# Four transposes in one PSUM bank, and maxima over partitions by way of DRAM, in a hybrid attention layer

## The chip, the cores and the metric

The kernel runs on one core of one Trainium2 chip. The metric is the device time of one execution in microseconds (us). Five instruction queues matter: TensorE (PE, with its weight loads as PEld), VectorE (DVE), ScalarE (ACT), GpSimd (POOL) and SyncE (SP). SP issues every DMA of this kernel. Each engine takes its own instructions in the order in which they stand.

## The reference

One layer of an encoder, applied to a prompt of 2048 rows ("p") and a sample of 512 rows ("s"), with 1024 features. Float32 inputs and outputs.

```
h    = RMSNorm(x) * (1 + scale(c)) + shift(c)
proj = h @ w_in                    # 1024 x 4096: q, k, v, gate of A (8 heads of 64) and of B
yA   = dilated_mixture(qA, kA, vA) * silu(gA)      # three dilated windows, mixed by their denominators
p    = softmax(qB kB / 8)          # two maps for each of 4 heads, every row against every row
oB   = (p[0] - lam * p[1]) @ vB
yB   = RMSNorm(oB) * g_sub * (1 - lam_init) * silu(gB)    # norm over one head's 128 values
y    = concat(yA, yB) @ w_out
out  = x + gate(c) * RMSNorm(y)
```

## The kernel before

**Precision.** Each operand of a large matmul is split into two float16 parts, and three products (high x high, high x low, low x high) are summed in PSUM. To split, an operand is first scaled by a power of two taken from its largest absolute value. That maximum has to be known on all 128 partitions. `allmax` (L175) finds it from a column of 128 partial maxima: TensorE transposes the column into a row in PSUM (L178), DVE takes the row's maximum (L180), TensorE multiplies it by a row of ones, which gives the value on all partitions (L182, two instructions in the trace), and `pow2` (L168 to L170) reads it out of PSUM. Both matmuls take a PSUM tile from the pool "pv".

Besides two calls for the modulation of h, `allmax` is called for each of eight blocks of w_in (`raw_scale`, L294 is its column), once for w_out (`wo_scale`), and once for each of five blocks of y (`y_scale`, L877 is its column): 14 calls.

**Units.** The layer is worked in eight units of 128 features, in the order B, A, B, A, B, A, B, A (`ORDER`). Each unit goes over five blocks of 512 rows, four of p and then s. In the trace the unit from 641 to 905 us is a B unit and that from 905 to 1083 an A unit. The projections of the next block or unit (L460, L534, L557) are woven into the attention of the present one. In the last unit the output projection of finished blocks (`out_proj`, L918) is woven in, and the rest of it follows at the end.

**A block of a B unit** is four items of 128 rows (`ItemB`, j = 0 to 3). `front` makes scores (L602, L608), scales them and takes the minimum (DVE, L611), exponentiates (ACT, L618), and forms the difference of the two softmax maps (L634, L636); SP transposes the result by DMA (L637, L645) into `at`. `tail2` is at x V (L656, 48 matmuls into one "pv" tile for the prompt), and ACT copies the result out (L663, L664) while POOL makes the norm's factor (L666 to L669). `tail3` scales o by that factor (ACT, L675), transposes it on TensorE into another "pv" tile (L677), and DVE multiplies by g_sub and the gate `sg` into `yt` (L681). At j = 3 `y_out` takes partial maxima (L571) and writes yt to DRAM (L573). While the units run, the pool "pv" has one buffer: `psum(1024, 3, 1, 1)`. Three items are in flight, so `tail3` of one item stands between matmuls of later ones.

**A block of an A unit** has eight items with smaller tiles. Exponentials are scaled and split on ACT and DVE (L745, L747) into four buffers "hl", SP transposes them by DMA (L748, L749), and TensorE multiplies (L765, L771) into a "pv" tile that ACT and DVE read (L779, L780).

**The order** is not that of the code alone: the tile framework's scheduler places the instructions of each engine ahead of the run, by its own estimate, and adds the waits. Each engine, SP too, then runs its list strictly.

Of the kernel before, what the change touches and what calls it, by code (L numbers as in the profile page):

```python
# [8 lines left out]
F32 = mybir.dt.float32  # L9
# [5 lines left out]
ALU = mybir.AluOpType  # L15
AX = mybir.AxisListType
# [3 lines left out]
P = 128  # L20
# [17 lines left out]
def hybrid_kernel(ctx, tc, x_p, x_s, w_in, w_ada, w_out, cvec, cols, lamv, gsub,  # L38
                  tab, m23, m1, ident, out_p, out_s):
    nc = tc.nc  # L40
# [8 lines left out]
    NU = len(ORDER)  # L49
# [42 lines left out]
    def PT(shape, tag):  # L92
        return T(PS[tag], shape, F32, tag)
# [5 lines left out]
    def nm(s):  # L99
        uid[0] += 1  # L100
        return f"{s}_{uid[0]}"
# [3 lines left out]
    def T(pool, shape, dt, tag, **kw):  # L105
        if tag in RARE:
            kw = {"bufs": 2}
        return pool.tile(shape, dt, tag=tag, name=nm(tag), **kw)
# [6 lines left out]
    V = nc.vector  # L115
# [49 lines left out]
    def pow2(e_out, inv_out, src, name):  # L165

        g = T(tn, [P, 1], F32, "p2")
        V.tensor_scalar_max(g, src, 1e-30)  # L168
        V.tensor_scalar(e_out.bitcast(I32), g.bitcast(I32), 0x7F800000, None, op0=ALU.bitwise_and)
        V.tensor_scalar(inv_out.bitcast(I32), e_out.bitcast(I32), 0x7F800000, None, op0=ALU.bitwise_xor)  # L170
# [4 lines left out]
    def allmax(col, tag="pv"):  # L175

        tp = PT([P, 512], tag)
        nc.tensor.transpose(tp[0:1, 0:P], col, id_sb)  # L178
        m = T(tn, [1, 1], F32, "am1")
        V.reduce_max(m, tp[0:1, 0:P], axis=AX.X)  # L180
        bc = PT([P, 512], tag)
        mm(bc[:, 0:1], lhsT=one_sb, rhs=m, start=True, stop=True)  # L182
        return bc[:, 0:1]

    RAW = {}

    def raw_load(n):
# [98 lines left out]
    def raw_scale(n):  # L286

        g, raw = ORDER[n], RAW[n]
        mg = T(tn, [P, 8], F32, "mg")
        for q in range(KT):  # L290
            V.tensor_reduce(mg[:, q:q + 1], raw[:, q, :], axis=AX.X, op=ALU.max, apply_absolute_value=True)
            yield 0.0
        ag = T(tn, [P, 1], F32, "ag")
        V.reduce_max(ag, mg, axis=AX.X)  # L294
        E = T(tn, [P, 1], F32, "E")
        S = C([P, 1], F32, f"wS{g}")
        pow2(E, S, allmax(ag), f"w{g}")
        smul(isw[:, g:g + 1], E, 2.0 ** -13)
        smul(S, S, 2.0 ** 12)
        WS[n] = S  # L300
        yield 0.0
# [266 lines left out]
    y_made = {}  # L568

    def y_out(r, g, c, y):  # L570
        V.tensor_reduce(yam[:, c + (r == "s") * NSB["p"], g:g + 1], y, axis=AX.X, op=ALU.max,  # L571
                        apply_absolute_value=True)
        nc.sync.dma_start(y_dram[r][c][:, g, :], y)  # L573
        y_made[r, c] = y_made.get((r, c), 0) + 1

# [2 lines left out]
    class ItemB:  # L580
# [67 lines left out]
        def tail2(self):  # L648
            r, g, c, j, st = self.a
            u = U[r, g]  # L650
            NT = SQ[r] // P
            Vv = u["V"]
            po = PT([P, 512], "pv")
            for i, (a, b) in enumerate(((self.ah, 0), (self.ah, 1), (self.al, 0))):
                for k in range(NT):
                    mm(po[:, :128], lhsT=a[:, k, :], rhs=Vv[:, k, 128 * b:128 * b + 128],  # L656
                       start=(k == 0 and i == 0), stop=(k == NT - 1 and i == 2))
                    if k % 4 == 3:
                        yield 0.23
            self.o = T(ev, [P, P], F32, "o")  # L660
            jk = T(ev, [P, P], BF16, "ojk", bufs=1)
            ss = T(tn, [P, 1], F32, "ss")
            act(jk, po[:, :128], AF.Square, accum_out=ss)  # L663
            act(self.o, po[:, :128], AF.Copy)  # L664
            v = T(tn, [P, 1], F32, "rv")
            nc.gpsimd.tensor_scalar(v, ss, u["k2"], EPS_T, op0=ALU.mult, op1=ALU.add)  # L666
            self.rst = T(tn, [P, 1], F32, "ro")
            nc.gpsimd.tensor_tensor(self.rst, v, mhalf, op=ALU.pow)
            nc.gpsimd.tensor_tensor(self.rst, self.rst, u["kb"], op=ALU.mult)  # L669
            yield 0.05  # L670

        def tail3(self):
            r, g, c, j, st = self.a
            u = U[r, g]
            act(self.o, self.o, AF.Copy, scale=self.rst)  # L675
            pt_ = PT([P, 512], "pv")
            nc.tensor.transpose(pt_[:, :128], self.o, id_sb)  # L677
            yield 0.1
            if "yt" not in st:
                st["yt"] = T(qp, [P, 4, P], F32, "yt")  # L680
            V.scalar_tensor_tensor(st["yt"][:, j, :], pt_[:, :128], gsub_sb, u["sg", c][:, j * P:(j + 1) * P],  # L681
                                   op0=ALU.mult, op1=ALU.mult)
            if j == 3:
                y_out(r, g, c, st["yt"].rearrange("p a b -> p (a b)"))

    def krange(r, c):

# [135 lines left out]
    def wo_scale():  # L823
        mg = T(tn, [P, 8], F32, "mg")
        for q in range(4):
            raw = T(wp, [P, 2, D], F32, "w")
            nc.sync.dma_start(raw, w_out[:, 2 * q:2 * q + 2, :])
            for i in range(2):
                V.tensor_reduce(mg[:, 2 * q + i:2 * q + i + 1], raw[:, i, :], axis=AX.X, op=ALU.max,
                                apply_absolute_value=True)  # L830
                yield 0.0
        ag = T(tn, [P, 1], F32, "ag")
        V.reduce_max(ag, mg, axis=AX.X)
        E = T(tn, [P, 1], F32, "E")
        wo["S"] = C([P, 1], F32, "woS")
        wo["i"] = C([P, 1], F32, "woi")
        pow2(E, wo["S"], allmax(ag), "wo")
        smul(wo["i"], E, 2.0 ** -13 * 2.0 ** -13)
        smul(wo["S"], wo["S"], 2.0 ** 12)
        yield 0.0  # L840
# [33 lines left out]
    def y_scale(r, c):  # L874

        ag = T(tn, [P, 1], F32, "ag")
        V.reduce_max(ag, yam[:, c + (r == "s") * NSB["p"], :], axis=AX.X)  # L877
        s = T(tn, [P, 4], F32, "ys")
        pow2(s[:, 0:1], s[:, 1:2], allmax(ag), "y")
        V.tensor_scalar(s[:, 0:1], s[:, 0:1], wo["i"], None, op0=ALU.mult)  # L880
        smul(s[:, 1:2], s[:, 1:2], 2.0 ** 12)
        V.tensor_scalar(s[:, 2:3], s[:, 0:1], s[:, 0:1], 1.0 / D, op0=ALU.mult, op1=ALU.mult)
        YS[r, c] = s

    def y_first(r, c, j):

        if j == 0:
            y_scale(r, c)
        s = YS[r, c]
        t = T(wp, [P, 8 * D], mybir.dt.uint8, "w")  # L890
        y32 = t[:, 0:4 * D].bitcast(F32)
        yh, yl = t[:, 4 * D:6 * D].bitcast(F16), t[:, 6 * D:8 * D].bitcast(F16)
        nc.sync.dma_start(y32.rearrange("p (k i) -> p k i", k=KT), y_dram[r][c][:, :, P * j:P * j + P])
        act(yh, y32, AF.Copy, scale=s[:, 1:2])
        V.scalar_tensor_tensor(yl, y32, s[:, 1:2], yh, op0=ALU.mult, op1=ALU.subtract)
        return yh.rearrange("p (k i) -> p k i", k=KT), yl.rearrange("p (k i) -> p k i", k=KT)
# [287 lines left out]
```

## Time and profile before

| | |
|---|---|
| median of 3 runs | 2182.41 us (2176.42 to 2187.44) |
| the profiled execution | 2191.28 us, of which its span is 2189.5 |
| PE busy in the span | 1910.8 us (87%) |
| DVE busy | 1541.1 us (70%) |
| ACT busy | 1152.7 us (53%) |
| DMA queue of SP, share of 16 engines | 73.6% |

How to read it: "busy" is the time in which an engine executes, and the gap before an instruction is put down to what released it last. Shares over the whole span hide that A and B units differ, so stretches of the span are read apart.

### The profile page before, as it was taken

How to read it: one execution, taken by the hardware profiler on the slowest of the kernel's cores; microseconds unless marked ns; L12 is line 12 of the kernel's file. 1: busy time of each engine (PE TensorE's matmuls, PEld its weight loads, DVE VectorE, ACT ScalarE, POOL GpSimd, SP SyncE). 2: the span in 40 equal slices, each digit the busy share in tenths (PEclk: the TensorE clock that was granted, in tenths of full speed). 3: DMA queues.
4: the chain of work that ended last, by engine and by line, in shares of the span. 5: the costliest groups of instructions: out<-in, count | busy, mean ns of one | idle time of the engine just before them, and what ended most of it. 6: DMA issues, size and time to landing. Idle time of an engine off the chain costs nothing. (4 is left out here: it accounts for less than half of the span.)

```text
span 2189.5 us, 47689 instructions
## 1 busy us (share of the span) xinstructions
PE 1910.8 (87%) x18545; PEld 1285.2 (59%) x18545; DVE 1541.1 (70%) x3428; ACT 1152.7 (53%) x2278; POOL 394.9 (18%) x1049
## 2 busy tenths in 40 slices
PE   4878997898989988888899888897989878989898
PEld 2665665666767666666566666574665554444443
DVE  3777998676669988666599886666888665455543
ACT  3555665555547666555467665554566644333321
POOL 0122222221112222111122221111222121100000
PEclk7789999999999999999999999898999888999999
DMA  7585787888857789898477888888776779665553
GB/s 293 171 253 126 138 163 149 188 158 165 186 130 152 145 196 188 140 173 192 114 151 145 184 188 155 170 183 235 147 148 157 159 163 191 122 133 126 130 163 111
DMA packets 726834, 360.12 MB, mean 164 GB/s; under 512 B 639808, under 2 KB 686672, under 8 KB 723152
## 3 DMA queue, kind: packets, MB, share of 16 engines
q1 hardware_dynamic: 726608, 357.08, 73.6%
q8 instruction: 145, 2.38, 0.5%
q14 instruction: 81, 0.66, 0.1%
HBM read 164.79 MB, written 36.97 MB: 92 GB/s over the span
## 5 line engine op out<-in xcount | busy, mean ns | idle before, releaser
L460 PE MATMUL pj<-w,h 128*128 128x256 f16 x3840 | 480.9, 281 | 29.1 <-DVE V L476 8.2
L460 PEld LDWEIGHTS <-h 128*128 128x128 f16 x3840 | 379.1, 101 | 103.9 <-issue 40.5
L618 ACT ACTIVATE pp<-sc,nb 128x1024 f32<-128x1024 f32 (+1 forms) x288 | 304.3, 1060 | 100.2 <-DVE sc L611 83.2
L534 PE MATMUL pj<-w,h 128*128 128x128 f16 x3840 | 257.1, 223 | 15.0 <-ACT q L541 8.5
L534 PEld LDWEIGHTS <-h 128*128 128x128 f16 x3840 | 231.6, 100 | 43.4 <-issue 32.5
L557 PE MATMUL pj<-h,w 128*128 128x512 f16 x960 | 230.7, 392 | 17.9 <-ACT q L541 17.9
L656 PE MATMUL pv<-V,at 128*128 128x128 f16 x3072 | 207.5, 227 | 38.1 <-DVE yt L681 29.0
L656 PEld LDWEIGHTS <-at 128*128 128x128 f16 x3264 | 201.9, 102 | 64.6 <-issue 47.8
L747 DVE SCALAR_TENSOR_TENSOR hl<-pp,Z,hl 128x640 f16<-128x640 f32 (+2 forms) x160 | 140.3, 881 | 119.4 <-DMA at<-hl 71.6
L443 POOL TENSOR_TENSOR rp<-q,tab_sb 128x64 f32<-128x64 f32 x160 | 67.3, 420 | 788.4 <-ACT q L466 469.5
L745 ACT ACTIVATE hl<-pp,Z 128x640 f16<-128x640 f32 (+2 forms) x160 | 130.3, 823 | 132.5 <-DMA at<-hl 108.7
L611 DVE TENSOR_SCALAR_CACHE_REDUCE sc<-sc,us,nb 128x1024 f32<-128x1024 f32 x128 | 172.3, 1346 | 37.1 <-PE sc L608 15.9
L611 DVE TENSOR_SCALAR_CACHE_REDUCE sc<-sc,us 128x1024 f32<-128x1024 f32 (+1 forms) x160 | 188.1, 1179 | 10.8 <-PE sc L608 10.2
L636 ACT ACTIVATE hl<-pp,rz 128x1024 f16<-128x1024 f32 (+1 forms) x144 | 155.6, 1095 | 60.7 <-issue 38.7
L731 ACT ACTIVATE pp<-pp,nb 128x640 f32<-128x640 f32 (+2 forms) x160 | 131.5, 822 | 105.9 <-DVE nb L726 100.1
L644 DVE SCALAR_TENSOR_TENSOR hl<-pp,rz,hl 128x1024 f16<-128x1024 f32 (+1 forms) x144 | 174.5, 1223 | 16.8 <-DMA at<-hl 5.9
L602 PE MATMUL sc<-K,Qc 128*128 128x512 f16 x512 | 158.6, 389 | 30.2 <-ACT pp L618 29.5
L557 PEld LDWEIGHTS <-w 128*128 128x128 f16 x960 | 94.1, 100 | 135.6 <-issue 42.0
L634 DVE SCALAR_TENSOR_TENSOR pp<-pp,rz,pp 128x1024 f32<-128x1024 f32 (+1 forms) x144 | 171.2, 1225 | 1.9
L918 PEld LDWEIGHTS <-w 128*128 128x128 f16 x960 | 92.9, 99 | 125.0 <-issue 17.0
L711 PE MATMUL sc<-K,Qc 128*32 128x512 f16 (+1 forms) x1024 | 119.2, 371 | 27.0 <-DMA Qc<-tq 17.1
L724 DVE CUSTOM_DVE_ANT_0 pp<-sc,maskp,us 128x384 f32<-128x384 f32 (+1 forms) x128 | 85.8, 678 | 71.0 <-PE sc L717 70.8
(200 smaller groups left out, 2843.9 us busy)
## 6 DMA issues: line engine op xcount, KB each, us to landing
h<-hp SPq DMA_DIRECT2D x124, 512.0 KB, 6.0
pp<-in_x_p_dram SPq DMA_DIRECT2D x32, 512.0 KB, 5.0
raw<-in_w_in_dram SPq DMA_DIRECT2D x8, 2048.0 KB, 8.1
h<-hs SPq DMA_DIRECT2D x32, 512.0 KB, 5.7
out_dram<-pp SPq DMA_DIRECT2D x20, 512.0 KB, 2.9
at<-hl SPq DMA_TRANSPOSE x608, 3.2
hp<-h SPq DMA_DIRECT2D x4, 2048.0 KB, 9.3
yp<-yt SPq DMA_DIRECT2D x32, 256.0 KB, 3.2
```

The costliest lines, as they stand in the source:

```text
L460: mm(ps[:, jj, :], lhsT=hT[:, a, k, j * P:(j + 1) * P], rhs=w[:, k, b, :], start=(k == 0 and i == 0), stop=(k == KT - 1 and i == 2))
L534: mm(ps[:, jj, 0:128], lhsT=hT[:, a, k, j * P:(j + 1) * P], rhs=w[:, k, b, 0:128], start=(k == 0 and i == 0), stop=(k == KT - 1 and i == 2))
L557: mm(ps, lhsT=w[:, k, b, 128:256], rhs=hT[:, a, k, :], start=(k == 0 and i == 0), stop=(k == KT - 1 and i == 2))
L602: mm(ps[:, n * 512:(n + 1) * 512], lhsT=Qc[:, j, m, 0, :], rhs=K[:, t:t + 4, m, :], start=True, stop=False)
L611: V.tensor_scalar(ps[:, :HW], ps[:, :HW], u["nsc"], nb[:, 0:1] if hf else 3e38, op0=ALU.mult, op1=ALU.min, accum_out=nb[:, hf:hf + 1])
L618: act(pt[m, hf][:, :HW], pss[hf][:, :HW], AF.Exp, scale=-1.0, bias=nb[:, NH - 1:NH], accum_out=Z[:, 2 * m + hf:2 * m + hf + 1])
L634: V.scalar_tensor_tensor(a, a, rz[:, 2:3], pt[0, hf][:, :HW], op0=ALU.mult, op1=ALU.add)
L636: act(hi[:, :HW], a, AF.Copy, scale=rz[:, 3:4])
L644: V.scalar_tensor_tensor(lo[:, :HW], a, sg, hi, op0=ALU.mult, op1=ALU.subtract)
L656: mm(po[:, :128], lhsT=a[:, k, :], rhs=Vv[:, k, 128 * b:128 * b + 128], start=(k == 0 and i == 0), stop=(k == NT - 1 and i == 2))
L731: act(sb[:, :NA], sb[:, :NA], AF.Exp, scale=-1.0, bias=nb[:, 1:2], accum_out=Z[:, 0:1])
L747: V.scalar_tensor_tensor(lo[:, :NA], sb[:, :NA], rz, hi[:, :NA], op0=ALU.mult, op1=ALU.subtract)
```

## The change

Three edits.

1. In a B block the four scaled o tiles of a block are kept in one buffer of 4 x 128 columns (one such buffer, where there were two of 128). At j = 3 all four are transposed into one "pv" tile, and one DVE instruction on 128 x 512 makes yt, where each item had its own transpose and its own DVE instruction on 128 x 128.
2. A second way to spread a maximum, `allmax_slow`: SP writes the column to DRAM, then reads it back as a row on all partitions, and DVE takes the row's maximum. It is used for seven of the eight blocks of w_in, for w_out and for the five blocks of y. The first w_in block and the modulation keep `allmax`.
3. `y_scale` is called when a block's last part of y is written, and not when its first output tile is begun; its result tile gets five buffers.

```diff
+    def allmax_slow(col):
+        d = dr.tile([P, 1], F32, tag=nm("amd"), name=nm("amd"))
+        nc.sync.dma_start(d, col)
+        row = T(tn, [P, P], F32, "amr", bufs=2)
+        nc.sync.dma_start(row, d.rearrange("p o -> (p o)").partition_broadcast(P))
+        m = T(tn, [P, 1], F32, "amc", bufs=2)
+        V.reduce_max(m, row, axis=AX.X)
+        return m
...
-        pow2(E, S, allmax(ag), f"w{g}")
+        pow2(E, S, (allmax if n == 0 else allmax_slow)(ag), f"w{g}")
...
         y_made[r, c] = y_made.get((r, c), 0) + 1
+        if y_made[r, c] == NU:
+            y_scale(r, c)
...
-            self.o = T(ev, [P, P], F32, "o")
+            if j == 0:
+                st["o"] = T(ev, [P, 4, P], F32, "o", bufs=1)
+            self.o = st["o"][:, j, :]
...
             act(self.o, self.o, AF.Copy, scale=self.rst)
-            pt_ = PT([P, 512], "pv")
-            nc.tensor.transpose(pt_[:, :128], self.o, id_sb)
-            yield 0.1
-            if "yt" not in st:
-                st["yt"] = T(qp, [P, 4, P], F32, "yt")
-            V.scalar_tensor_tensor(st["yt"][:, j, :], pt_[:, :128], gsub_sb, u["sg", c][:, j * P:(j + 1) * P],
-                                   op0=ALU.mult, op1=ALU.mult)
             if j == 3:
-                y_out(r, g, c, st["yt"].rearrange("p a b -> p (a b)"))
+                pt_ = PT([P, 4, P], "pv")
+                for q in range(4):
+                    nc.tensor.transpose(pt_[:, q, :], st["o"][:, q, :], id_sb)
+                yield 0.4
+                yt = T(qp, [P, 512], F32, "yt")
+                V.scalar_tensor_tensor(yt, pt_.rearrange("p a b -> p (a b)"), gsub_sb, u["sg", c],
+                                       op0=ALU.mult, op1=ALU.mult)
+                y_out(r, g, c, yt)
+            yield 0.0
...
-        pow2(E, wo["S"], allmax(ag), "wo")
+        pow2(E, wo["S"], allmax_slow(ag), "wo")
...
-        s = T(tn, [P, 4], F32, "ys")
-        pow2(s[:, 0:1], s[:, 1:2], allmax(ag), "y")
+        s = T(tn, [P, 4], F32, "ys", bufs=5)
+        pow2(s[:, 0:1], s[:, 1:2], allmax_slow(ag), "y")
...
-        if j == 0:
-            y_scale(r, c)
         s = YS[r, c]
```

The changed code has other line numbers: L693 is its transpose (L677 before), L668 its at x V (L656), L188 and L190 the two new DMAs. The scheduler reorders much around the edits. On TensorE, in the second B unit, at the end of the third block (fourth item), it had before:

```order
L460 LDWEIGHTS h_10044
L460 MATMUL pj_11514<-w_6687,h_10044 128x256
L677 MATMUL pv_11140<-id_sb,o_11090 128x128
L656 LDWEIGHTS at
L656 MATMUL pv_11185<-V_5369,at 128x128
```

At the same place it has now:

```order
L693 MATMUL pv_11064<-id_sb,o_10425 128x128 x3
L567 LDWEIGHTS w_4729
L567 MATMUL pj_11159<-h_9982,w_4729 128x512
...
L693 MATMUL pv_11064<-id_sb,o_10425 128x128
L567 LDWEIGHTS w_4729
...
L614 LDWEIGHTS Qc_9995
L614 MATMUL sc_11041<-K_5324,Qc_9995 128x512
...
L668 LDWEIGHTS at
L668 MATMUL pv_11113<-V_5325,at 128x128
```

The next item's at x V stood directly behind the transpose; now projections (17 matmuls of L567 before the fourth transpose, seven after it) and eight score matmuls stand between. In the 20 B blocks the four transposes stand at the end of a block alone.

On SP, in the first B unit, where the sample's keys and values (Ks, Vs) of the next unit are stored, it had before:

```order
L645 DMA_TRANSPOSE at<-hl_4422 128x8x128
L491 DMA_TRANSPOSE Ks_1786<-tk_4666 128x2x128 x2
L494 DMA vbs_124<-Vs_1789 128x2x256
L637 DMA_TRANSPOSE at<-hl_4461 128x8x128
L637 DMA_TRANSPOSE at<-hl_4465 128x8x128
```

and has now (L657, L649 and L504 are the L645, L637 and L494 of before):

```order
L657 DMA_TRANSPOSE at<-hl_4395 128x8x128
L504 DMA vbs_124<-Vs_1789 128x2x256
L501 DMA_TRANSPOSE Ks_1786<-tk_4631 128x2x128 x2
L188 DMA amd_6177<-ag_6173 128x1
L190 DMA amr_6179<-amd_6177 128x128
L381 DMA h_4702<-hp_112 128x2048 x4
L649 DMA_TRANSPOSE at<-hl_4430 128x8x128
```

The read of `amd` stands directly behind its write, and the loads of h and the next transposes for `at` stand behind both. In the last unit, when the first block of y is complete, SP had:

```order
L573 DMA yp_116<-yt_26393 128x512
L518 DMA V_4002_26766<-vbp_123 32x5x256
L911 DMA pp_26791<-in_x_p_dram 128x1024
L748 DMA_TRANSPOSE at<-hl_26820 128x6x128
L893 DMA w_26787<-yp_116 128x8x128
L893 DMA w_26799<-yp_116 128x8x128
```

and has now (L583 and L906 are the L573 and L893 of before):

```order
L583 DMA yp_116<-yt_26213 128x512
L188 DMA amd_26564<-ag_26561 128x1
L381 DMA h_26970<-hs_115 128x2048 x2
L906 DMA w_26607<-yp_116 128x8x128
L190 DMA amr_26566<-amd_26564 128x128
L906 DMA w_26619<-yp_116 128x8x128
```

The write of the column goes out right behind that of y, and its read behind the load of the first y tile.

## Rows read from the trace of the kernel before

**Rows 1.** The page, part 1: engine, busy us, share, instructions.
```profile
PE 1910.8 (87%) x18545; PEld 1285.2 (59%) x18545; DVE 1541.1 (70%) x3428; ACT 1152.7 (53%) x2278; POOL 394.9 (18%) x1049
```
**Rows 2.** Windows: length, busy time of five engines, granted clock, DMA share, GB/s.
```profile
655.00:816.00 161.00, 149.18 (x1514) 104.61 (x1514) 149.85 (x246) 107.86 (x212) 42.39 (x103) 0.99 0.79 160
1724.00:1781.00 57.00, 44.53 (x461) 34.67 (x460) 41.85 (x80) 33.47 (x73) 16.04 (x37) 0.88 0.73 154
905.00:1083.00 178.00, 152.15 (x1835) 112.68 (x1832) 109.09 (x315) 88.49 (x169) 23.27 (x77) 0.94 0.80 167
814.00:817.40 3.40, 3.34 (x32) 3.34 (x32) 2.53 (x6) 2.04 (x3) 0.00 (x0) 0.51 1.21 260
```
**Rows 3.** Groups by line: busy us, mean ns | idle before, releasers.
```profile
L656 PE MATMUL pv<-V,at 128*128 128x128 f16 x3072 | 207.5, 227 | 38.1 <-DVE yt L681 29.0 <-DMA at<-hl 9.0
...
L681 DVE SCALAR_TENSOR_TENSOR yt<-pv,gsub_sb,sg 128x128 f32<-128x128 f32 x80 | 27.6, 344 | 9.4 <-PE pv L677 9.4
L562 DVE SCALAR_TENSOR_TENSOR sg<-sg,pj 128x512 f32<-128x512 f32 x40 | 27.3, 682 | 29.9 <-ACT sg L561 29.8
...
L677 PE MATMUL pv<-id_sb,o 128*128 128x128 f32 x80 | 24.1, 302 | 17.3 <-ACT o L675 17.2
...
L656 PE MATMUL pv<-Vs,at 128*128 128x128 f16 x192 | 14.0, 225 | 3.9 <-DVE yt L681 3.9
```
**Rows 4.** Timeline, 803 to 816 us: start, us, instruction, [idle before <-releaser].
```profile
803.56 4.83 DVE L291 TENSOR_REDUCE mg<-raw 128x1 f32<-128x512 f32 x8
...
813.68 0.33 DVE L681 SCALAR_TENSOR_TENSOR yt<-pv,gsub_sb,sg 128x128 f32<-128x128 f32 x1
...
814.06 2.19 PE L656 MATMUL pv<-V,at 128*128 128x128 f16 x19 [4.57 <-DVE yt L681]
```
**Rows 5.** Groups by line, the two matmul lines of `allmax`.
```profile
L182 PE MATMUL pv<-am,one_sb 1*128 1x1 f32 x28 | 5.7, 270 | 3.0 <-DVE am L180 3.0
...
L178 PE MATMUL pv<-id_sb,ag 128*1 128x128 f32 x14 | 4.2, 300 | 18.1 <-DVE ag L294 10.6 <-DVE yt L780 4.4 <-DVE ag L877 3.0
```
**Rows 6.** Timeline, 46 to 48 us, PE: the first w_in block's call.
```profile
46.44 0.37 PE L178 MATMUL pv<-id_sb,ag 128*1 128x128 f32 x1 [9.58 <-DVE ag L294]
...
47.19 0.58 PE L182 MATMUL pv<-am,one_sb 1*128 1x1 f32 x2 [0.37 <-DVE am L180]
```
**Rows 7.** Chain that ended last: start us, us, what.
```profile
2087.90 0.11 PE pv L178
...
2092.97 0.31 PE pv L182 x2
```
**Rows 8.** Waits of SP's queue: us in total, times, longest.
```profile
SPq L518 <- DMA vbp<-V: 8.8, 5, 3.1
```
**Rows 9.** DMA issues: KB each, median us to landing.
```profile
V<-vbp SPq DMA_DIRECT2D x64, 80.0 KB, 2.5
...
gsub_sb<-in_gsub_dram SPq DMA_DIRECT2D x1, 0.5 KB, 2.7
gg<-hl SPq DMA_DIRECT2D x1, 8.0 KB, 1.3
```
**Rows 10.** Line L518: ns min/median/max of one issue on SP, first and last start.
```profile
L518 SPq DMA_DIRECT2D V<-vbp x64: 312/435/912, 415.4 to 1911.2; - x64
```
**Rows 11.** Waits of all engines: us in total, times, longest.
```profile
ACT hl L745 <- DMA at<-hl: 108.7, 59, 4.5
...
DVE hl L747 <- DMA at<-hl: 71.6, 38, 7.1
...
PE pv L765 <- DMA at<-hl: 12.3, 12, 3.8
```
**Rows 12.** Timeline, 1844 to 1857 us: the first tile of the output projection.
```profile
1854.46 1.15 ACT L894 ACTIVATE w<-w,ys 128x1024 f16<-128x1024 f32 x1 [4.92 <-DMA w<-yp]
...
1855.66 1.03 PE L918 MATMUL pj<-raw,w 128*128 128x512 f16 x2 [6.07 <-ACT w L894]
```

## The prediction

> **What bounds the kernel now.** I read part 1 of the page first. TensorE is busy 87% of the span, DVE 70%, ACT 53% [rows 1]. That makes TensorE the first suspect, but B and A units differ, so the windows come next. In 161 us of the second B unit PE and DVE are both busy for 93% (149.2 and 149.9 us) [rows 2]: there they share the limit, and a wait that leaves one of them is worth something only as far as the other can follow. In a block of the last B unit neither is full (44.5 and 41.9 of 57 us), and in an A unit PE has 152 of 178 us and DVE 109 [rows 2]: there PE waits for chains.
>
> Then I read what PE waits for, in the groups by line. In front of at x V it waits 29.0 us (prompt) and 3.9 us (sample) for DVE's L681, which empties the only "pv" bank, and in front of the transpose L677 17.2 us for ACT's scaling of o [rows 3]. The timeline shows one such wait: the next at x V starts at 814.06, 4.57 us late, 0.05 us after L681 has ended; DVE had come to L681 only at 813.68, behind other work, a group of eight reductions of 4.83 us among it [rows 4]. So this wait is also DVE being behind, not only a bank too few.
>
> **Edit 1, the B blocks.** DVE runs L681 80 times at 344 ns, 27.5 us. Instead it runs 20 instructions on 128x512. The nearest row is L562, the same operation on 128x512 with one operand in PSUM: 682 ns [rows 3], 13.6 us for 20. DVE saves 13.9 us. ACT's and POOL's work stays, and so do the 80 transposes, which run four at a time.
>
> On PE, the waits for L681 and for o are 29.0 + 3.9 + 17.2 = 50.1 us. Where one transpose in four blocks the bank, three quarters of these have no instruction left to wait: 37.6 us. The last quarter may shrink too, since the order now puts 7 projection and 8 score matmuls between the fourth transpose and the next at x V where nothing stood before. What is late next is the DVE work of the scores (L611) with ACT's exponentials behind it, which fill those 93%.
>
> The bounds are 0 (each wait comes back as a wait for DVE) and -37.6 us. Where DVE is full the gain is what DVE saves, and most B blocks are like that, so I stay near that row: -14 us, and 2 more for the last B unit, where both engines have room. Term: **-16 us**. The single o buffer costs nothing: item 0 of the next block writes it after its own at x V, which stands behind the four transposes on PE anyway.
>
> **Edit 2, what leaves TensorE.** Thirteen of 14 calls go. Their waits on PE are 18.1 + 3.0 us less those of the first w_in block, which keeps its call (9.58 + 0.37): 11.2 us [rows 5, 6]. In the chain a call takes 0.11 + 0.31 us of PE's time [rows 7], 5.5 us for thirteen. So the most is -16.7 us; the least is 0, if PE stands before the next score tile instead. DVE's own reduction changes little (one of 1x128 for one of 128x128). I take half: **-8 us**.
>
> **Edit 2, what comes onto SP and DVE.** Thirteen writes and thirteen reads join SP's queue. No row shows a write of four bytes per partition to DRAM. The nearest wait on SP is that for stored values before they are read back (L518), 8.8 us in 5 times, 1.8 us each, 3.1 at most [rows 8]; landings of small transfers are 1.3 us (8 KB written) and 2.7 us (4 bytes per partition, read) [rows 9]. At 1.8 us a pair holds SP for 23 us in thirteen; 26 issues at 0.435 us [rows 10] are 11 more. Together 34 us of SP.
>
> Behind a held SP stand the loads of h and the transposes for `at`, for whose landing at x V waits. How much reaches PE? In A units ACT and DVE already wait 108.7 + 71.6 us for such transposes to free "hl", while PE waits 12.3 us for them [rows 11]: about 7%. Bounds 0 and +34; I take one part in seven: **+5 us**, more than those 7%, because B units have no such slack.
>
> The Trainium skill (DMA: Bandwidth & Descriptors, Anatomy of one DMA) speaks against this edit: a DMA has a fixed cost of about 2.0 us, most of it the receipt of the write, heaviest for DRAM, and a wait for it sits on the issuing sequencer. By that figure, as an estimate, the thirteen pairs hold SP for 26 us in place of 23, and the sum would be half a microsecond higher.
>
> DVE then waits for the row. From the column to the row it is 1.8 + 2.5 us (landing of V<-vbp, rows 9) and two issues, 5.2 us. In B units DVE's order puts some 4 to 5 us of other instructions between; in the five calls for y only a few short ones, so up to 4 us each is open, in a unit in which DVE has room. Bounds 0 and +20: **+2 us**.
>
> **Edit 3** costs nothing: the first tile of the output projection is held by the load of y, which ended ACT's wait at 1854.46, and PE waited 6.07 us for it [rows 12]. The column's trip starts right behind the write of y and lands under the same load. At the end of the program the last block's scale is needed long after it is begun.
>
> **The sum.** -16 - 8 + 5 + 2 = -17 us, from the profiled execution's 2191.28 us to 2174.3. The runs' median, 2182.41, is 8.9 us under that execution; the same difference from it gives **2165 us**.
>
> **Rivals.** *More is gained.* PE's waits go in full and nothing fills them. For: the last B unit has room on both engines. Against: DVE's 93% in the second. It would be -38 - 17 + 5 + 2 = -48 us. There is also the clock: in the 3.4 us after the wait of 4.57 us PE was granted 0.51 of its speed, which is 1.2 GHz of 2.4 [rows 2, 4], so half of that stretch's work came late, about 1.7 us for one wait; four such waits fewer give some 7 us. Time: 2182 - 55 = 2127 us. The skill's rule (TensorE: Matmul & The Clock Gate, HAM oscillation) says the same, that a matmul stream which waits runs its next stretch at half rate; by that rule the gain of a removed wait is larger than the wait.
>
> *Nothing comes of it.* DVE stays the limit in B units and its 13.9 us turn up as its own waits for PE and ACT; half is left, 7 us, TensorE's calls give 3, SP takes 8: 2180 us. For: 4.57 us of waiting was DVE's backlog [rows 4]. Against: fewer instructions on a full engine should show.
>
> *Slower: the trip through DRAM holds two in-order queues.* In the order, six of the thirteen reads stand directly behind their write, with loads of h or transposes for `at` behind them, and DVE's reduction stands before score work. Its whole price is 34 us on SP and 20 on DVE, 54; the gains taken above are 24. Slower by more than the bound below needs 35 of the 54, two thirds, to reach PE. At 70% it is 38 - 24 = +14: 2196 us. For: DMA share is 0.8 in B and A units alike [rows 2], so small transfers land late. Against: 12.3 us of 180 reach PE now [rows 11]. That the change doesn't do what it says is no rival: the order shows both edits.
>
> **How the numbers follow.** Forecast 0.45, more 0.17, nothing 0.24, slower 0.14. About 0.5% (10.9 us: under 2171.5, over 2193.3) is what a measurement of this kernel can tell from no change. The forecast's own range is 2150 to 2177: the gains of edits 1 and 2 half-way to their upper bounds (-27 and -12) or half-way to nothing (-8 and -4), with SP and DVE at +7; four fifths of it are faster. Faster: 0.36 + 0.17 and 0.07 of "nothing" give 0.60; slower: 0.14; the rest, 0.26, is within 0.5%. For 8 times in 10 the range leaves out the far part of both outer rivals: 2132 to 2195.
>
> **What would show it.** Right: the wait of at x V for the DVE instruction that makes yt falls from 33 to under 12 us, the transposes' wait for o from 17 to under 6, that DVE line takes about 13.6 us in 20 instructions, and the B units shorten by 3 to 5 us each. The wait of SP for its own column's landing is near 1.8 us in thirteen. Wrong: the waits go but "scores wait for ACT" or "DVE waits for PE" grow by as much (nothing); SP's wait is 3 us or more, and at x V's wait for `at` doubles from its 21 us (slower); PE's granted clock rises in B units (more).

## The result, and the profile after

The changed kernel takes **2301.48 us** (median of 4 runs, 2294.64 to 2303.41); the kernel before, beside it on the same chip, 2182.86. The ratio is 1.054, with a 95% interval of 1.0506 to 1.0575: 118.6 us slower, where 17 us faster was forecast and 2195 us was the top of the range. Of the rivals, the slower one named the trip through DRAM, which is the larger part of the loss; its price was too small, and it did not name what edit 1 costs.

The page of the changed kernel, part 1 (engine, busy us, share, instructions), against [rows 1]:

```profile
span 2299.8 us, 47563 instructions
PE 1932.4 (84%) x18506; PEld 1288.3 (56%) x18506; DVE 1541.1 (67%) x3368; ACT 1150.3 (50%) x2278; POOL 391.2 (17%) x1049
```

The span grew by 110.3 us. TensorE does 39 matmuls fewer and is busy 21.6 us more; the other 88.7 us are idle time. DVE's busy time is the same to a tenth of a us, although the durations of its instructions add up to 1748.4 us in place of 1760.3: they overlap less. So no work came on top that an engine would show: the time is waiting. The windows of the changed kernel say the same of the stretch in which PE and DVE had both been full (length, busy time of PE, PEld, DVE, ACT, POOL, granted clock, DMA share, GB/s):

```profile
655.00:816.00 161.00, 144.22 (x1373) 95.58 (x1369) 137.04 (x213) 101.29 (x198) 40.51 (x93) 0.96 0.70 137
```

149.2 and 149.9 us there [rows 2] have become 144.2 and 137.0, with 141 matmuls fewer done in the same 161 us. Neither engine is full any more. None of the thirteen writes to DRAM falls into this stretch (the nearest are at 612.8 and 855.2 us), so this drop is not the trip's.

The groups by line of the changed kernel (busy us, mean ns | idle before, releasers). L668 is at x V, L780 that of A units, L693 the transposes, L696 the DVE instruction that makes yt, L192 the new reduction:

```profile
L668 PE MATMUL pv<-V,at 128*128 128x128 f16 x3072 | 230.4, 228 | 92.4 <-DMA at<-hl 81.2 <-ACT pp L630 10.1 <-DVE tq L559 0.2
...
L693 PE MATMUL pv<-id_sb,o 128*128 128x128 f32 x80 | 16.1, 288 | 4.7 <-ACT o L689 2.6 <-ACT o L678 2.1
L696 DVE SCALAR_TENSOR_TENSOR yt<-pv,gsub_sb,sg 128x512 f32<-128x512 f32 x20 | 14.9, 743 | 2.2 <-PE pv L693 2.2
...
L192 DVE TENSOR_REDUCE amc<-amr 128x1 f32<-128x128 f32 x13 | 3.7, 286 | 117.2 <-DMA amr<-amd 117.2
```

Against [rows 3]: the wait of at x V for yt, 32.9 us, is gone altogether, the transposes' wait for o fell from 17.2 to 2.6, and yt costs 14.9 us in 20 instructions. All of that was forecast. But in front of at x V now stand 81.2 us for `at`, the tile that SP transposes by DMA, where 9.0 had stood. Its busy time rose as well, from 207.5 to 230.4 us at the same mean of one: its matmuls overlap less. Its weight loads, which are pieces of `at`, wait too (PEld L668 below). These 22.9 us are as much as TensorE's whole 21.6; its other groups rose and fell by up to 10 us each, which nearly cancels.

The waits of all engines in the changed kernel (us in total, times, longest), against [rows 11]:

```profile
PEld L668 <- DMA at<-hl: 120.5, 89, 9.9
...
DVE amc L192 <- DMA amr<-amd: 117.2, 13, 16.8
...
PE pv L668 <- DMA at<-hl: 85.4, 58, 9.4
...
PE pv L780 <- DMA at<-hl: 54.3, 25, 8.3
```

The waits of SP's queue, with the same columns, and the DMA issues (KB each, median us to landing), against [rows 8, 9]:

```profile
SPq L190 <- DMA amd<-ag: 78.6, 11, 8.3
```

```profile
at<-hl SPq DMA_TRANSPOSE x608, 3.2
...
amr<-amd SPq DMA_DIRECT2D x13, 64.0 KB, 4.7
amd<-ag SPq DMA_DIRECT2D x13, 0.5 KB, 8.3
```

The write of 512 bytes takes longer to land (8.3 us) than 8 KB had taken (1.3). How one trip looks, in the last unit: the timeline of SP in the changed kernel (start us, us, instruction), and then that of DVE.

```profile
2152.33 0.53 SPq L188 DMA_DIRECT2D amd<-ag  x1
2159.75 0.32 SPq L190 DMA_DIRECT2D amr<-amd  x1
2160.17 1.18 SPq L763 DMA_TRANSPOSE at<-hl  x1
```

```profile
2156.37 0.62 DVE L762 SCALAR_TENSOR_TENSOR hl<-pp,Z,hl 128x384 f16<-128x384 f32 x1 [0.15 <-ACT hl L760]
2164.31 0.29 DVE L192 TENSOR_REDUCE amc<-amr 128x1 f32<-128x128 f32 x1 [7.32 <-DMA amr<-amd]
```

For 7.4 us SP issues nothing, with a transpose for `at` queued behind the read. The trip takes 12 us from the write's issue to the reduction, and DVE, which had come to it 7.32 us early, holds its next instructions for as long.

### The profile page after: what moved, and what is told of

Its sections match the earlier page's. It is cut to its first block, busy times and chain, and to the rows that moved or that the text cites. A ratio compares the mean times of both kernels' runs of the same rounds, so it can differ in the third digit from the quotient of the medians.

```text
span 2299.8 us, 47563 instructions
## 1 busy us (share of the span) xinstructions
PE 1932.4 (84%) x18506; PEld 1288.3 (56%) x18506; DVE 1541.1 (67%) x3368; ACT 1150.3 (50%) x2278; POOL 391.2 (17%) x1049
## 5 line engine op out<-in xcount | busy, mean ns | idle before, releaser
L470 PE MATMUL pj<-w,h 128*128 128x256 f16 x3840 | 471.2, 278 | 35.7 <-DVE Vs L486 9.4
L668 PE MATMUL pv<-V,at 128*128 128x128 f16 x3072 | 230.4, 228 | 92.4 <-DMA at<-hl 81.2
L668 PEld LDWEIGHTS <-at 128*128 128x128 f16 x3264 | 207.2, 103 | 151.3 <-DMA at<-hl 120.5
L544 PE MATMUL pj<-w,h 128*128 128x128 f16 x3840 | 265.9, 224 | 14.5 <-ACT q L551 5.5
L567 PE MATMUL pj<-h,w 128*128 128x512 f16 x960 | 224.0, 386 | 13.9 <-ACT q L551 13.9
L614 PE MATMUL sc<-K,Qc 128*128 128x512 f16 x512 | 163.8, 399 | 37.0 <-ACT pp L630 31.3
L656 DVE SCALAR_TENSOR_TENSOR hl<-pp,rz,hl 128x1024 f16<-128x1024 f32 (+1 forms) x144 | 174.0, 1223 | 13.9 <-DMA at<-hl 6.5
L567 PEld LDWEIGHTS <-w 128*128 128x128 f16 x960 | 93.3, 99 | 125.7 <-issue 29.3
```

The lines of the kernel that those rows point to most:

```text
L470: mm(ps[:, jj, :], lhsT=hT[:, a, k, j * P:(j + 1) * P], rhs=w[:, k, b, :], start=(k == 0 and i == 0), stop=(k == KT - 1 and i == 2))
L544: mm(ps[:, jj, 0:128], lhsT=hT[:, a, k, j * P:(j + 1) * P], rhs=w[:, k, b, 0:128], start=(k == 0 and i == 0), stop=(k == KT - 1 and i == 2))
L567: mm(ps, lhsT=w[:, k, b, 128:256], rhs=hT[:, a, k, :], start=(k == 0 and i == 0), stop=(k == KT - 1 and i == 2))
L614: mm(ps[:, n * 512:(n + 1) * 512], lhsT=Qc[:, j, m, 0, :], rhs=K[:, t:t + 4, m, :], start=True, stop=False)
L656: V.scalar_tensor_tensor(lo[:, :HW], a, sg, hi, op0=ALU.mult, op1=ALU.subtract)
```

## The experiments

Two theories stood first. A: nearly all of the 118 us is the trip through DRAM. B: the four transposes cost time as well, because at x V had been paced by the "pv" tile that passed once per item. Within A: what DVE waits for (A1) against what SP's queue is held for (A2). Times are medians, ratios are to the kernel before, measured beside each run, with 95% intervals.

**The four transposes alone.** Edit 1 stays; all maxima go by TensorE and `y_scale` is back in `y_first`.

```diff
-        pow2(E, S, (allmax if n == 0 else allmax_slow)(ag), f"w{g}")
+        pow2(E, S, allmax(ag), f"w{g}")
...
```

> Edit 1 alone (four transposes at a time), every maximum by way of TensorE as before. Theory A (the trip through DRAM is what costs, its write lands after 7 us and more, and DVE and SP stand still for it): this kernel is without the trip, so it is not slower than before; by the terms of the prediction 2160 to 2175 us, and at x V waits for the transposes into at no more than before (some 21 us). Theory B (the new order of the B blocks is what costs, at x V stands too early in it): slower than before by half of the 118 us or more, 2240 us and up, with at x V waiting 60 us or more for at.

2209.93 us, 1.0127 (1.0092 to 1.0162): edit 1, forecast at -16 us, costs 27 us by itself. That lies between the two forecasts (A up to 2175 us, B from 2240); B's sign, 60 us or more of waiting for `at`, came, so B holds for this part of the loss and not for half of it. Its waits:

```profile
PE pv L666 <- DMA at<-hl: 79.5, 53, 4.5
...
DVE sc L621 <- PE sc L618: 67.1, 49, 4.5
...
PE pv L666 <- DVE yt L694: 3.1, 6, 1.0
```

The 33 us for yt went, and 79.5 us for `at` came, without a single trip through DRAM. DVE waits longer for scores too; the kernel before has, in the same view:

```profile
DVE sc L611 <- PE sc L608: 26.0, 21, 5.2
```

And in the window 655 to 816 us the drop of the changed kernel is here in full:

```profile
655.00:816.00 161.00, 142.56 (x1394) 95.58 (x1392) 137.62 (x213) 100.90 (x199) 40.60 (x96) 0.96 0.70 137
```

**The trip alone.** Edits 2 and 3 stay, each item has its own transpose and DVE instruction again.

```diff
-            if j == 3:
-                pt_ = PT([P, 4, P], "pv")
...
+            pt_ = PT([P, 512], "pv")
+            nc.tensor.transpose(pt_[:, :128], self.o, id_sb)
...
```

> Edits 2 and 3 alone (maxima by way of DRAM, y's scale early), one transpose per item as before. Theory A: slower than before by about the whole 118 us, 2290 to 2315 us, with DVE waiting some 110 us in 13 times for the row. Theory B: slower by less than half of it, under 2240 us.

2280.4 us, 1.0455 (1.0428 to 1.0483): 98 us. With the 27 of edit 1 that is 125 where both together give 119, so the two add up nearly. It is ten under the range that A gave and far over B's. Of its waits:

```profile
DVE amc L192 <- DMA amr<-amd: 124.3, 13, 14.2
...
PE pv L777 <- DMA at<-hl: 53.5, 25, 8.4
```

**Edit 1 with the transposes back per item.** One wide buffer for o is kept, the transposes and the DVE instruction are per item.

```diff
+            pt_ = PT([P, 512], "pv")
+            nc.tensor.transpose(pt_[:, :128], self.o, id_sb)
...
+            V.scalar_tensor_tensor(st["yt"][:, j, :], pt_[:, :128], gsub_sb, u["sg", c][:, j * P:(j + 1) * P],
+                                   op0=ALU.mult, op1=ALU.mult)
             if j == 3:
-                pt_ = PT([P, 4, P], "pv")
-                for q in range(4):
-                    nc.tensor.transpose(pt_[:, q, :], st["o"][:, q, :], id_sb)
...
```

> As the run of edit 1 alone, which took 2210 us, but each item transposes its own o into its own bank and DVE reads it per item again; the one wide buffer for o stays. Theory B1 (without a transpose per item in the only bank, at x V stands so early in the order that it waits for the DMA transposes): the bank paces at x V again, its wait for at falls from 80 us to some 10, and the time goes back to 2175 to 2195 us. Theory B2 (the single o buffer is what holds it up): the time stays at 2200 us or more.

2182.91 us, 1.0002 (0.9984 to 1.0019). The single o buffer costs nothing, as forecast: in the traces every engine has the same list as before. So the transposes per item bring the old order back, and with it the waits of before:

```profile
PE pv L666 <- DVE yt L693: 33.6, 16, 4.6
...
PE pv L666 <- DMA at<-hl: 10.7, 12, 2.3
```

**A gate of one column.** Edit 1 as it is, and for the first three items of a block TensorE transposes one column of o into a "pv" tile, of which DVE reads one value. It does no work that the result needs; it takes the "pv" tile once per item.

```diff
+            if j < 3:
+                gt_ = PT([P, 512], "pv")
+                nc.tensor.transpose(gt_[0:1, 0:P], self.o[:, 0:1], id_sb)
+                gate = T(tn, [1, 1], F32, "gate", bufs=2)
+                V.tensor_scalar_mul(gate, gt_[0:1, 0:1], 1.0)
```

> As the run of edit 1 alone, plus a gate: items 0 to 2 transpose one column of o into the only bank and DVE reads one value of it, so that the bank again passes once per item from at x V to the transpose and back. Theory B1 (pacing by the bank): at x V's wait for at falls from 80 us to under 30 and the time to 2170 to 2190 us, DVE keeping most of its saving of 14 us. Theory B2 or a cost of the four-wide transpose itself: 2200 us or more.

2173.71 us, 0.9962 (0.994 to 0.9984): 36 us faster than edit 1 alone with more instructions, and the one version that is faster than both kernels, by 0.4% against the kernel before. Its waits:

```profile
PE pv L666 <- DMA at<-hl: 8.8, 10, 1.7
...
PE pv L666 <- DVE gate L692: 5.9, 7, 2.5
```

and its window, with both engines near full again:

```profile
655.00:816.00 161.00, 148.75 (x1497) 104.60 (x1495) 146.56 (x244) 106.16 (x210) 42.10 (x100) 0.98 0.82 166
```

So the pacing was worth what edit 1 lost. How it worked can be counted in the trace, in the order in which TensorE's matmuls start: those that stand between an item's last score matmul and the start of its at x V, 80 items.

| kernel | matmuls between, median | PE's wait at x V for `at`, us |
|---|---|---|
| before | 207 | 9.0 |
| four transposes alone | 145 | 79.5 |
| one transpose per item, wide o | 207 | 10.7 |
| gate of one column | 198.5 | 8.8 |
| at x V later in the code (below) | 146.5 | 74.3 |
| the changed kernel | 127.5 | 85.4 |

In that stretch ACT, POOL, DVE and SP make `at` from the scores. With fewer matmuls in it, TensorE arrives first and waits.

**At x V later in the code.** Edit 1, with `tail2` moved one place later among the parts of an item and `tail3` after it.

```diff
                 if x == "mid":
-                    if p2:
+                    if isinstance(p3, ItemB):
+                        yield from p3.tail3()
+                    if isinstance(p2, ItemA):
                         yield from p2.tail2()
-                    if isinstance(p2, ItemA):
                         yield from p2.tail3()
...
                     if isinstance(p2, ItemB):
-                        yield from p2.tail3()
+                        yield from p2.tail2()
```

> As the run of edit 1 alone, but at x V of an item is put half an item later in the program (behind the next item's exponentials), and the scaling and transposes half an item later as well. Theory B1 (at x V stands too early): its wait for at falls from 80 us to under 30, and the time is 2150 to 2190 us. If the landing itself has become later (SP held up), the wait stays above 60 us and the time above 2200.

2225.55 us, 1.0192 (1.0166 to 1.0217): no remedy, a miss. The table says why the waits stayed: the scheduler put at x V at the same distance from its scores as without the move (146.5 matmuls, 145). That it was 16 us slower than edit 1 alone was not followed up.

**The trip issued by POOL.** The changed kernel with both DMAs on another queue. If SP's held queue were the cost, most of it would go.

```diff
-        nc.sync.dma_start(d, col)
+        nc.gpsimd.dma_start(d, col)
...
-        nc.sync.dma_start(row, d.rearrange("p o -> (p o)").partition_broadcast(P))
+        nc.gpsimd.dma_start(row, d.rearrange("p o -> (p o)").partition_broadcast(P))
```

> The changed kernel with the two DMAs of each trip issued by GpSimd and not by SP, so SP no longer waits for the column's landing. Theory A1 (DVE's waits for the row are the loss): the time stays within 25 us of the changed kernel's 2301, since DVE still waits for the same trip. Theory A2 (SP standing still, with the transposes behind it, is the loss): half of the loss or more goes, 2240 us or less, and at x V's wait for at falls from 140 us to under 60.

2307.57 us, 1.0576 (1.0549 to 1.0604): nothing gained, which by the text above speaks for A1, DVE's wait. SP no longer waits, POOL does (116.0 us in 13), and TensorE waits as much for `at`:

```profile
PE pv L668 <- DMA at<-hl: 87.1, 65, 6.4
```

The transposes' landings say how. The 21 that SP issued from 1.5 us ahead of such a write to 7 us behind it landed after 9.8 us in the median, the other 587 after 3.2 us. It is not the place in the program that is slow: near the writes of 512-byte rows (last run below), 28 transposes in the same interval landed after 3.3 us. So the write holds up transfers of another queue, and what is held lies behind both queues. That POOL's standing still costs what SP's did is not excluded by this run alone. The Trainium skill (DMA: Bandwidth & Descriptors, Issuing engines are not separate DMA queues) says that DMAs of all engines end up on the same 16 DMA engines; this run agrees.

**Landings in the quiet.** The kernel before, with 20 pairs of a write to DRAM and a read back behind its last work. Only their landings are read. A fifth kind, 512 bytes from one partition, is left out of the cut.

```diff
+    for _ in range(4):
+        nc.sync.dma_start(q1, src[:, 0, 0:1])        # 4 bytes per partition, neighbours
+        nc.sync.dma_start(back, q1.rearrange("p o -> (p o)").partition_broadcast(P))
...
+        nc.sync.dma_start(q2, src[:, 0, 0:16])       # 64 bytes per partition
...
+        nc.sync.dma_start(q3, src[:, 0, 0:P])        # 512 bytes per partition
...
+        nc.sync.dma_start(q3[:, 0:1], src[:, 0, 0:1])   # 4 bytes, 512 apart
...
```

> The kernel before, with 20 pairs of write to DRAM and read back added after the last output work, each pair waiting for the one before; only the landings are of interest. Four pairs each of: 4 bytes per partition into one run of 512 bytes (as in the change); 64 bytes per partition; 512 bytes per partition; 4 bytes per partition, 512 bytes apart in DRAM; 512 bytes from one partition. Theory A' (the write of 4 bytes to neighbouring addresses is slow by itself): about 7 us for the first, 2 to 3 us for those of 64 and 512 bytes per partition. Theory A'' (it is the queue in front of it, other transfers being ahead on the same rings): all five land in 1.5 to 3 us in the quiet.

The answers by line (ns min/median/max of the issue, first and last start; then the landing), in the order of the four writes; of the four issues of a line the view knows two to four landings:

```profile
L1107 SPq DMA_DIRECT2D q<-w x4: 319/320/336, 2150.6 to 2190.0; - x4
DMA to landing us min/median/max: 7.6/7.7/9.2
...
L1110 SPq DMA_DIRECT2D q<-w x4: 319/320/425, 2151.0 to 2215.0; - x4
DMA to landing us min/median/max: 1.4/1.4/8.0
...
L1113 SPq DMA_DIRECT2D q<-w x4: 319/320/430, 2151.5 to 2230.9; - x4
DMA to landing us min/median/max: 1.5/1.5/1.5
...
L1116 SPq DMA_DIRECT2D q<-w x4: 319/320/320, 2235.2 to 2249.1; - x4
DMA to landing us min/median/max: 1.4/1.4/1.4
```

So the 8 us are no queue in front of the write: it takes 7.6 and 7.7 us with little else under way (9.2 is the one with a store of the output beside it). Nor is it that each partition sends 4 bytes: 512 bytes apart they land in 1.4 us. It is 128 values of 4 bytes side by side. The 8.0 of L1110 is the one issued 0.37 us behind such a write (2151.00 behind 2150.63): it landed with it, for the read that waits for that write was issued at 2158.84 and this one landed at 2159.04. For the same 512 bytes from one partition the view has no landing; the read that waits for it was issued 1.1 us behind it. The read behind the 4-byte neighbours (L1108) takes 4.4 to 4.7 us too, where that behind 64-byte rows takes 3.1 and that behind 512-byte rows 2.8.

**The trip, unused.** Edit 1 alone, and behind each of thirteen columns a write and a read whose row nobody uses. DVE doesn't wait for a row and TensorE keeps its matmuls: SP's held queue and the transfers themselves (A2) are left.

```diff
+    def allmax_and_trip(col):
+        d = dr.tile([P, 1], F32, tag=nm("amd"), name=nm("amd"))
+        nc.sync.dma_start(d, col)
+        row = T(tn, [P, P], F32, "amr", bufs=2)
+        nc.sync.dma_start(row, d.rearrange("p o -> (p o)").partition_broadcast(P))
+        return allmax(col)
...
```

> As the run of edit 1 alone (maxima by TensorE), with the thirteen trips through DRAM issued by SP as in the change but used by nobody: SP is held for the write's landing, DVE waits for nothing. Theory A1 (DVE's wait for the row is most of the loss): within 30 us of 2210 us. Theory A2 (SP being held is most of it): 2265 us or more, that is more than half of the 91 us by which the changed kernel is over edit 1 alone.

2282.84 us, 1.0462 (1.0432 to 1.0492): 73 us over edit 1 alone, of the 92 that the changed kernel is over it. So most of the price is paid on the DMA side without anyone using the row. That is A2's range, and the run on POOL's queue met A1's: neither is the whole, since the write costs whichever queue it stands in. The other 19 are the net of DVE's wait for the row, the matmuls that leave TensorE, edit 3 and another order; these were not separated.

**The same with rows of 64 bytes.** DVE spreads the column over 16 values first, and the write has 64 bytes per partition.

```diff
-        d = dr.tile([P, 1], F32, tag=nm("amd"), name=nm("amd"))
-        nc.sync.dma_start(d, col)
+        d = dr.tile([P, 16], F32, tag=nm("amd"), name=nm("amd"))
+        wide = T(tn, [P, 16], F32, "amw", bufs=2)
+        V.tensor_copy(wide, col.to_broadcast([P, 16]))
+        nc.sync.dma_start(d, wide)
...
```

> As the run of the unused trip (2283 us, 73 over edit 1 alone), but each partition writes 64 bytes and not 4, to a run of its own; the read, the count of DMAs and SP's wait for the landing stay. Theory A3 (the write of 4 bytes to neighbouring addresses lands late, and what is queued behind it on the shared DMA engines with it): the write lands in 2 to 3 us, and the time falls to 2210 to 2230 us. If it is the number of DMAs and of waits: 2265 us or more.

2235.71 us, 1.0231 (1.0196 to 1.0266): 47 of the 73 us are gone with sixteen times the bytes, six short of the range that A3 gave; the 26 that are left were not followed up. The scheduler's order is another too, so the 47 hold a change of order as well. The wait of SP's queue is 18.8 us in 8 times where it was 84.9 in 12, and its issues:

```profile
amr<-amd SPq DMA_DIRECT2D x13, 64.0 KB, 3.3
amd<-amw SPq DMA_DIRECT2D x13, 8.0 KB, 2.4
```

**The write without the read.** As the unused trip, with the read left out, so that SP waits for nothing.

```diff
-        row = T(tn, [P, P], F32, "amr", bufs=2)
-        nc.sync.dma_start(row, d.rearrange("p o -> (p o)").partition_broadcast(P))
```

> As the run of the unused trip, but without its read: the thirteen writes of 4 bytes per partition remain, and no instruction of SP waits for them. Theory A3 (the write holds the DMA engines for every transfer behind it): most of the 73 us stays, 2250 us or more, and transposes issued within 7 us behind a write land after 6 to 12 us against 3.2 elsewhere. Theory A2 (SP standing still for the landing): the time falls to 2210 to 2230 us.

2248.59 us, 1.0294 (1.0261 to 1.0326): 39 of the 73 us come from the write alone, which nobody waits for. That is just under the 2250 named above: about half, and not most of it. One of its waits shows how, at 10.4 us at the longest where edit 1 alone had 4.5:

```profile
PE pv L671 <- DMA at<-hl: 79.1, 40, 10.4
```

The twelve transposes issued up to 7 us behind a write landed after 6.5 us in the median (2.8 to 13.6), the others after 3.2. The four loads of h issued 0.6 to 2.0 us behind the write at 848.9 us landed after 12.2 to 15.5 us; four issued 0.4 to 1.8 us behind a write of 64-byte rows (the run before this one, at 379.1 us) after 5.2 to 8.8. The rest of the 73, some 34 us, is the read and SP's wait in front of it: but for the read, the two traces have the same lists on every engine. These two were not separated.

**The changed kernel with rows of 512 bytes.** The column is spread over 128 values, the write has 512 bytes per partition, and the row read back is partition 0's, so the maximum over the other partitions is left out.

```diff
-        d = dr.tile([P, 1], F32, tag=nm("amd"), name=nm("amd"))
-        nc.sync.dma_start(d, col)
+        d = dr.tile([P, P], F32, tag=nm("amd"), name=nm("amd"))
+        wide = T(tn, [P, P], F32, "amw", bufs=1)
+        V.tensor_copy(wide, col.to_broadcast([P, P]))
+        nc.sync.dma_start(d, wide)
...
-        nc.sync.dma_start(row, d.rearrange("p o -> (p o)").partition_broadcast(P))
+        nc.sync.dma_start(row, d[0, :].partition_broadcast(P))
```

> The changed kernel, but each partition writes 512 bytes (its maximum 128 times), and the row that is read back is that of partition 0 alone, so the maximum over the other partitions is left out; count and order of DMAs and of DVE's waits stay. Theory A3: the write lands in 2 to 3 us, DVE's waits for the row fall from 117 to under 50 us, and the time is 2215 to 2240 us, edit 1's loss of 27 us and a rest. If the trip's two DMAs are slow for their number: 2270 us or more.

2220.52 us, 1.0174 (1.0149 to 1.02): 81 of the 119 us are gone, with the same number of DMAs, the same waits in the program and 128 times the bytes written. Here too the scheduler's order is another, so the 81 hold more than the landing. Of its waits, and its issue:

```profile
DVE amc L194 <- DMA amr<-amd: 32.7, 10, 12.9
```

```profile
amd<-amw SPq DMA_DIRECT2D x13, 64.0 KB, 3.4
```

DVE's wait for the row was 117.2 us in the changed kernel. What is left over edit 1 alone is 10.6 us.

## Why the prediction was wrong

**Edit 1, -16 us, measured +27.** Each thing counted in the step came: DVE's line at 14.9 us for a forecast 13.6, the wait for yt under 12 us (0), that for o under 6 (2.6). But the saving on DVE's line did not shorten DVE's busy time in the changed kernel. What failed is the sentence "What is late next is the DVE work of the scores", and with it the lower bound of 0. The next late thing was `at`, which this step did not look at. The one "pv" tile, taken at x V, for the transpose and again, was a cost of 33 us and also what kept 207 matmuls between scores and at x V. Free of it, the scheduler took the matmuls from between (145), though it knows `at` only by its own estimate, and the DMA transposes landed too late. Two experiments show it from both sides: per-item transposes give the old order and 2183 back, and a gate that passes the tile along gives 2174 with edit 1 otherwise whole. That the cause is an estimate of the scheduler that is too short for these transposes was not tried; the distances were counted and the waits measured. The forecast "B units shorten by 3 to 5 us each" failed with it: between the last maxima of y of one unit and the next, the second and third B unit took 284 and 286 us in place of 263 and 263 (the last one 250 in place of 276, but the A unit behind it 315 in place of 260). With edit 1 alone, without a trip, they took 271 and 269, the last one 248 and the A unit behind it 283.

The size of the hope was not absurd. With pacing kept the edit gives -8 us (0.9962), half of the -16. The prediction's order of instructions did show what happened: between the transposes and at x V stood new work, and what had stood between scores and at x V was not counted.

**Edit 2, on TensorE, -8 us.** Not separated. It is one of the parts of the 19 us that the changed kernel is over the unused trip.

**Edit 2, on SP and DVE, +5 and +2 us, measured 92 together with the gain on TensorE.** The step that failed is "At 1.8 us a pair holds SP": the price was taken from the wait for stores of V [rows 8], beside an 8 KB write and a read of 4 bytes per partition [rows 9]. The write that came is of another kind, 7.2 to 12.8 us to land, and SP stood 78.6 us in eleven times, 7.1 us each. The trip took 12 us where 5.2 were worked out, so DVE waited 117 us in 13 times, 9 each, where "up to 4 us" was left open.

Even with the landing right, the sum lacked a term: the write holds back the transfers behind it, on its own queue and on another. That is 39 of the 73 us (the write alone), and it fits that another queue changed nothing. TensorE's waits for `at`, 9.0 + 12.3 us before, are 85.4 + 54.3; the share that reaches TensorE was put at one part in seven, from 7% read in A units, where the transposes have slack, and it was no small share.

The Trainium skill (DMA: Bandwidth & Descriptors, Anatomy of one DMA), whose figure of about 2.0 us the prediction weighed, gives it for DMAs that GpSimd issues. On SP's queue, rows of 64 and 512 bytes came near it: 1.4 and 1.5 us in the quiet, 2.4 and 3.4 in use. It does not fit 4-byte neighbours, 7.7 us. Where page and measurement differ, the measurement decides. The same page (Specifications) warns that under 512 bytes a transfer is a read and a write; here 64-byte rows and 4 bytes at a stride of 512 were as fast as 512-byte rows, so size alone is not what costs. That neighbours in one short stretch are written one after another would fit (6.3 us more for 128 of them, about 50 ns each, an estimate from these landings), and was not tried apart.

**Edit 3, nothing.** It was in the trip-alone kernel with edit 2 and was not tried by itself.

**The rivals.** "The trip through DRAM holds two in-order queues" had both its signs come true: SP's wait for the column's landing over 3 us (7.1) and at x V's wait for `at` more than doubled (21 to 140). Its price of 54 us was too low: 98 were measured in the trip-alone kernel. Its mechanism, a held queue, is a part of it only: the write alone, for which no queue stands still, costs 39. And its chance of 0.14 leaned on a row of another shape of transfer. The sign of "Nothing comes of it", DVE's waiting for PE, came in part (26.0 to 67.1 us for scores with edit 1 alone), beside a larger wait that it did not name. "More is gained" had the clock for it; the mean granted clock instead fell from 0.942 to 0.931.

## What to carry to other kernels

A wait for a buffer can be what keeps a statically scheduled order in step: before removing it, count what stands between each producer and its consumer in the list, in both kernels, and look at the longest chain that this distance covers, here scores to exponentials to DMA transposes. A DMA's price is its shape: if the trace has no row with the same bytes per row on the same side, bound it from above by several times the nearest one (here 7.1 us of SP's waiting came for 1.8) and ask what is queued behind it, on every queue.

## What the runs showed of the hardware

A write of 128 neighbouring values of 4 bytes, one from each partition, landed in DRAM after 7.7 us in the quiet, and a read of it took 4.6. As 64-byte rows the same column landed after 1.4 us, as 512-byte rows after 1.5, as 4 bytes 512 apart after 1.4. While the write of 4-byte neighbours was under way, other transfers landed with it or behind it, from the same queue (8.0 us in place of 1.4) and from another (9.8 us in place of 3.2). No run tells why such a write is slow.

Open: how the 34 us of the read and of SP's wait divide, why moving at x V in the code cost 16 us more, and what keeps 26 us on the unused trip with rows of 64 bytes and 10.6 us on the change with rows of 512.
